# Rotary queries split in the projections and fetched into the operand's two tiles; five softmax buffers instead of six

## The chip, the cores and the metric

The kernel runs on one core of a Trainium2 chip. The metric is the device time of one execution in microseconds (us); lower is better. TensorE (PE) multiplies matrices, VectorE (DVE), ScalarE (ACT) and GpSimd (POOL) do the elementwise work, SyncE (SP) mostly issues transfers. Transfers can be issued from the queues of SP, ACT and POOL, and each engine works its own list of instructions in order; semaphores tie the lists together.

## The reference

One inference step of two decoder layers: the even layer mixes pooling and retention, the odd layer is multi-head latent attention, each is followed by a gated feed-forward network with a short convolution. There are 1024 prompt positions and 8 sample sequences of 4 new positions (1056 columns in all), model width 1024. The change concerns the attention layer: 8 heads, of which every query has a part of 128 without position and a rotary part of 64. The latent cache of a sample sequence holds 8192 old positions in 64 pages, and pages are found by a table. For the prompt, `q_pe` and `k_pe` are the rotary parts and `c_kv` the latent:

```
q_nope, q_pe, c_kv, k_pe = mla_project(...)      # rope on q_pe and k_pe
k_nope, v = c_kv @ w_uk, c_kv @ w_uv             # per head
s = (q_nope . k_nope + q_pe . k_pe) * MLA_SCALE   # causal
out = softmax(s) @ v, then w_o
```

For the samples the same sum runs over the cached pages, with `w_uk` folded into the query: scores against the 256 latent and 64 rotary columns of every cached row, softmax, and the latent rows weighted by it.

## The kernel before

The program is written by a planner in Python. Each piece of work is a generator (`heads`, `scores`, `outs`, `prepare`, `keys`, `values` and so on) that issues instructions and yields what it needs next: an event (`ev`), a buffer out of a stock (`res`), data that is ready (`rd`). `Pipe.run` (L470 on) keeps a clock model and always lets the task run that has the best priority among those that could start. So the instruction lists of all engines follow from the plan, and an edit that changes a stock, an event or a modelled cost moves other instructions too. A tile framework then adds the semaphores; transfers from SP and ACT share eight completion semaphores, taken in turn, and a transfer waits until the earlier one on its semaphore has landed.

Numbers of 32 bits are multiplied in two parts: `split` writes a rounded (high) part by a ScalarE cast and the rest (low) by a VectorE subtraction; a product then takes high x high, high x low and low x high. For the rotary queries the two parts are stacked: the operand `q2` of 128 rows holds the high part in rows 0 to 63 and the low part in rows 64 to 127.

*Projections* (`mla_proj`, about 1340 to 1410 us). `rotary(g)` makes the rotary queries of heads 4g to 4g+3: for three chunks of 352 columns it multiplies with the up-projection, rotates on VectorE and POOL and leaves the two halves of the rotary dimension in two tiles of `z`. Then, per head and half, the ACT queue stores 32 rows of 1056 columns into a DRAM tile `qpd` of 64 x 8 x 1056 (8 stores for each g, 16 in all, 132 KB each), because the rows of a head have to come to other partitions. `plain` makes the parts without position.

*Attention* (`attention`, about 1410 to 1990 us) runs two streams together. The samples: 352 page loads on SP and 160 gathers on POOL bring keys (`kt`), 128 gathers bring values (`vt`); products with them carry L632. The prompt, head by head: `heads` makes the keys of head h from `w_ukv` (loaded for every two heads, ACT queue), `scores` makes the scores of a block of queries, takes the maximum, the exponential (`p<-sc,amx` on ACT) and the scale (`p<-p,asm` on DVE); `outs` transposes p (L638), copies the transposed pieces to `th` and multiplies with `vv`. All 128 x 1024 buffers of this stream (p, raw weights, raw queries) come out of one ring of NP = 6 tiles, tag "p".

The rotary queries of head h come in `heads`: once head h-1 has been scored, a buffer of the ring is taken, two ACT-queue loads bring `qpd[:, h]` twice (rows 0 to 63 and again 64 to 127), the task waits until they are there, ACT casts all 128 rows into `q2`, and DVE overwrites rows 64 to 127 with the difference. At the start `load_queries` fetches those of head 0 (`qpe0`) and the last 32 columns of all heads (`qraw`) from SP's queue; DVE copies the latter into `qpS`, the rotary queries of the samples. L405 is the line of a helper that records every operation other than products, L616 that of the wide product.

Of the kernel before, what the change touches and what calls it, by code (L numbers as in the profile page):

```python
# [7 lines left out]
F32 = mybir.dt.float32  # L8
F32R = mybir.dt.float32r
# [8 lines left out]
SEQ = 1024  # L18
# [35 lines left out]
NP = 6  # L54
LAG = 1000.0
PL = 2
# [505 lines left out]
class Kernel:  # L562
# [727 lines left out]
    def mla_proj(self, src):  # L1290
# [130 lines left out]
        def rotary(g):  # L1421
# [4 lines left out]
            for c in range(3):  # L1426
# [15 lines left out]
                nc.gpsimd.tensor_tensor(o2[:, t0:t0 + n], o2[:, t0:t0 + n], ta, ALU.add)  # L1442
            self.done(("uqp", g))
            for hh in range(4):
                for half, o in ((0, o1), (1, o2)):
                    nc.scalar.dma_start(self.qpd[half * 32:half * 32 + 32, g * 4 + hh], o[hh * 32:hh * 32 + 32])
# [22 lines left out]
    def attention(self):  # L1469
# [9 lines left out]
        for shape, dtype, tag, bufs in (  # L1479
# [3 lines left out]
                ([128, 4, RW], F32, "mx", None), ([128, SEQ], F32R, "q2", 1),  # L1483
# [16 lines left out]
        ukv0, qpe0 = ptile(), ptile()  # L1500
        nc.sync.dma_start(ukv0, io["w_ukv"][0])
        nc.gpsimd.memset(qpS, 0.0)
        qraw = ptile()[:, :MH * NS].rearrange("p (h t) -> p h t", h=MH)

        def load_queries():

            for e in range(2):
                nc.sync.dma_start(qraw[64 * e:64 * e + 64], self.qpd[:, :, SEQ:])
            for e in range(2):
                nc.sync.dma_start(qpe0[64 * e:64 * e + 64], self.qpd[:, 0, :SEQ])  # L1510
            for e in range(2):
                s = slice(64 * e, 64 * e + 64)
                nc.vector.tensor_copy(qpS[s, :, e].rearrange("p b h i -> p h b i"), qraw[s].rearrange("p h (b i) -> p h b i", b=NB))
# [209 lines left out]
        pipe.stock("p", NP - 5)  # L1723
        hs = {}

        def heads():

            for h in range(MH):
                if h % 2 == 0:
                    if h:  # L1730
                        yield ("res", "p", 1)
                        raw = ptile()
                        nc.scalar.dma_start(raw, io["w_ukv"][h // 2])
                    else:
                        raw = ukv0
                    yield ("rd", raw)
# [25 lines left out]
                if h:  # L1762
                    yield ("res", "p", 1)
                    raw = ptile()
                    for e in range(2):
                        nc.scalar.dma_start(raw[64 * e:64 * e + 64], self.qpd[:, h, :SEQ])
                    yield ("rd", raw)
                else:
                    raw = qpe0
                q2 = ap.tile([128, SEQ], F32R, tag="q2", name="q2", bufs=1)  # L1770
                nc.scalar.copy(q2, raw)
                nc.vector.tensor_tensor(q2[64:128], raw[64:128], q2[64:128].bitcast(F32), ALU.subtract)
                pipe.give("p")
# [241 lines left out]
```

## Time and profile before

| | us |
|---|---|
| median of 3 runs | 2918.33 |
| lowest, highest | 2912.61, 2920.26 |
| profiled execution | 2925.62 |
| its span | 2923.8 |
| TensorE busy in the span | 2762.6 |
| attention, about 1410 to 1990 | 580 |

The span lies 1.8 us below its execution's time, and that execution is 7.3 us above the median. The mean granted TensorE clock of the span is 0.968 of full speed. In the rows, a start in us stands first, then a length, and in brackets the idle time of that engine just before, with what ended it.

### The profile page before, as it was taken

To read this page: it belongs to the slowest core of one execution; us is meant where nothing else is said; L and a number is where in the kernel's file an instruction comes from. 1 tells how busy PE (TensorE), PEld (TensorE's weight loads), DVE (VectorE), ACT (ScalarE), POOL (GpSimd) and SP (SyncE) were. 2 spreads that over 40 slices of the span, in tenths; PEclk is the share of its full clock that TensorE was granted. 3 is DMA by queue.
4 is the path that set the end of the run, shared out by engine and by line. 5 is a ranking of instruction groups with operands and counts; after the bars stand their busy time and mean duration, and the time that the engine had idled before them with its cause. 6 is when DMAs were issued, how large, how long until landed. Compare 5 with 4: busy or idle time off the path is not lost.

```text
span 2923.8 us, 44128 instructions
## 1 busy us (share of the span) xinstructions
PE 2762.6 (94%) x16897; PEld 2469.5 (84%) x16897; DVE 1421.2 (49%) x2720; ACT 868.1 (30%) x1833; POOL 755.0 (26%) x787
## 2 busy tenths in 40 slices
PE   8999998999999999899898988899889999999997
PEld 6777997999999999889654544478889999999996
DVE  4444547544444444764352534444674444444446
ACT  3322435211211222343332323243442211211224
POOL 1222334010111011323455665413420110111102
PEclk9999999999999999999998999889999999999997
DMA  3111421110211111122789999724211111111101
GB/s 135 60 59 46 117 82 34 55 47 30 66 44 44 44 51 46 44 99 83 244 291 298 334 348 347 266 95 146 73 44 37 51 51 29 63 47 44 51 25 60
DMA packets 136275, 301.81 MB, mean 103 GB/s; under 512 B 20960, under 2 KB 84240, under 8 KB 135936
## 3 DMA queue, kind: packets, MB, share of 16 engines
q1 hardware_dynamic: 89472, 175.35, 18.5%
q0 software_dynamic: 27968, 98.00, 9.6%
q10 hardware_dynamic: 18624, 25.63, 2.9%
q8 instruction: 134, 2.20, 0.3%
q14 instruction: 77, 0.63, 0.1%
HBM read 283.71 MB, written 15.21 MB: 102 GB/s over the span
## 4 chain that ended last, share of the span: by engine, by line
PE 79%; DVE 6%; DMA 5%; issue 5%; ACT 2%; POOL 2%; SPq 1%; ACTq 0%; DVEq 0%; POOLq 0%
PE bank L616 71%; PE bank L632 4%; DMA kt<-in_kT 3%; PE sc L616 2%; PE bank L638 2%; DVE ln_v L405 1%; DVE x L405 1%; DVE z L405 1%; DMA kt<-in_kT,kix 1%; DMA p<-qpd 1%; SPq L405 1%; DMA vt<-in_vrow,vix 1%; SPq L1914 1%; POOL z L405 1%; DVE wl L405 1%
## 5 line engine op out<-in xcount | busy, mean ns | idle before, releaser
L616 PE MATMUL bank<-x,wh 128*128 128x352 f32 x5664 | 1380.0, 327 | 19.3 <-DVE x L405 18.1
L616 PEld LDWEIGHTS bank<-x,wh 128*128 128x128 f32 x5664 | 992.8, 190 | 33.9 <-DVE x L405 23.3
L616 PE MATMUL bank<-x,wl 128*128 128x352 f32 x2832 | 915.2, 323 | 7.1 <-DVE wl L405 7.1
L616 PEld LDWEIGHTS bank<-x,wl 128*128 128x128 f32 x2832 | 537.4, 190 | 8.6 <-DVE wl L405 8.2
L405 ACT CAST wh<-wr 128x1024 fp32r<-128x1024 f32 (+1 forms) x196 | 202.6, 1041 | 668.7 <-PE bank L616 638.5
L405 DVE SCALAR_TENSOR_TENSOR z<-z,bank 128x352 f32<-128x352 f32 (+3 forms) x440 | 219.7, 513 | 326.7 <-PE bank L616 313.9
L616 PE MATMUL bank<-ah,wh 128*128 128x352 f32 (+3 forms) x1088 | 353.0, 324 | 0.0
L616 PE MATMUL bank<-ah,wl 128*128 128x352 f32 (+3 forms) x1088 | 350.9, 323 | 0.0
L616 PE MATMUL bank<-al,wh 128*128 128x352 f32 (+3 forms) x1088 | 350.6, 322 | 0.0
L405 POOL TENSOR_TENSOR wl<-wr,wh 128x1024 fp32r<-128x1024 f32 (+1 forms) x61 | 147.8, 2430 | 636.8 <-PE bank L616 391.6
L405 DVE TENSOR_TENSOR wl<-wr,wh 128x1024 fp32r<-128x1024 f32 (+1 forms) x137 | 175.7, 1284 | 147.2 <-ACT wh L405 142.5
L616 PE MATMUL bank<-wh,x 128*128 128x512 f32 (+3 forms) x720 | 239.5, 394 | 8.2 <-ACT wh L405 8.2
L616 PEld LDWEIGHTS bank<-ah,wh 128*128 128x128 f32 x1088 | 207.9, 191 | 1.2
L616 PEld LDWEIGHTS bank<-al,wh 128*128 128x128 f32 x1088 | 207.7, 191 | 1.2
L616 PEld LDWEIGHTS bank<-ah,wl 128*128 128x128 f32 x1088 | 207.9, 191 | 0.6 <-DVE wl L405 0.6
L405 POOL DMA_INDIRECT kt<-in_kT,kix x160 | 158.8, 992 | 133.3 <-DMA kt<-in_kT 53.4
L405 POOL COPY co<-a 128x2 f32<-128x2 f32 x44 | 39.2, 891 | 553.5 <-ACT a L405 553.5
L405 DVE SCALAR_TENSOR_TENSOR y<-a,prm,y 128x352 f32<-128x352 f32 (+1 forms) x264 | 166.1, 629 | 9.8
L405 DVE TENSOR_TENSOR g<-y,bank 128x352 f32<-128x352 f32 (+2 forms) x176 | 71.6, 427 | 202.7 <-PE bank L616 201.6
L405 DVE TENSOR_SCALAR y<-a,prm 128x352 f32<-128x352 f32 x132 | 79.1, 599 | 183.1 <-ACT a L405 177.6
L616 PEld LDWEIGHTS bank<-wh,x 128*128 128x128 f32 (+1 forms) x720 | 127.9, 182 | 32.6 <-ACT wh L405 8.2
L405 POOL DMA_INDIRECT vt<-in_vrow,vix x128 | 124.1, 970 | 102.7 <-PE bank L632 60.5
(234 smaller groups left out, 3215.9 us busy)
## 6 DMA issues: line engine op xcount, KB each, us to landing
kt<-in_kT SPq DMA_DIRECT2D x352, 160.0 KB
wr<-in_w_up SPq DMA_DIRECT2D x88, 512.0 KB
wr<-in_w_dn SPq DMA_DIRECT2D x44, 512.0 KB
wr<-in_w_h SPq DMA_DIRECT2D x16, 512.0 KB
wr<-in_w_oe SPq DMA_DIRECT2D x16, 512.0 KB
wr<-in_w_om SPq DMA_DIRECT2D x16, 512.0 KB
z<-in_xT SPq DMA_DIRECT2D x12, 352.0 KB
z<-in_xT ACTq DMA_DIRECT2D x3, 1408.0 KB
```

The source lines that it names most:

```text
L405: r = f(*args, **kw)
L616: self.nc.tensor.matmul(out, lhsT, rhs, start=start, stop=stop)
L632: self.nc.tensor.matmul(out[32 * g:32 * g + m], lhsT, rhs, start=start, stop=stop, tile_position=(0, 32 * g))
L638: self.nc.tensor.transpose(out, in_, self.ident[:in_.shape[0], :in_.shape[0]])
L1914: reg = nc.sync.value_load(entry, min_val=0, max_val=last)
```

## The change

`rotary(g)` now splits each rotated chunk at once: ACT casts and DVE subtracts, two times per chunk, into two tiles each of `xh` and `xl` (tiles of the activations that stand free there, whose memory the pools of attention take over later). The stores go from these, high rows into `qpd` rows 0 to 63 and low rows into 64 to 127; `qpd` is 128 x 8 x 1056 and there are 16 stores for each g, 32 in all, of 132 KB each. In attention, `load_q2(h)` is one ACT-queue load of 128 x 1024 straight into the operand `q2`, which has two buffers. The load for head 0 is issued when the task starts, that of head h+1 when head h begins. The cast, the subtraction, the raw buffer and the planner's wait are gone. `qraw` takes high and low parts (four loads of 64x8x32 instead of two), and DVE adds them into `qpS` instead of copying. The ring has five tiles, one of which is free at the start as before, and the planner lets the cast of a later `w_ukv` start 6000 ns after the time at which its model has the load ready (UKV).

```diff
--- before.py
+++ after.py
@@ -51,8 +51,9 @@
 NEV = 3
 PAIRS = (0, 1, 2, 3)
 NTH = 2
-NP = 6
+NP = 5
 LAG = 1000.0
+UKV = 6000.0
 PL = 2
 LNX = -1000.0
 SX = 400.0
@@ -1440,10 +1441,15 @@
                 self.drop(2)
                 nc.gpsimd.tensor_tensor(o1[:, t0:t0 + n], o1[:, t0:t0 + n], tb, ALU.subtract)
                 nc.gpsimd.tensor_tensor(o2[:, t0:t0 + n], o2[:, t0:t0 + n], ta, ALU.add)
+                yield True
+                for half, o in ((0, o1), (1, o2)):
+                    self.split(self.xh[:, 4 + 2 * g + half, t0:t0 + n], self.xl[:, 4 + 2 * g + half, t0:t0 + n], o[:, t0:t0 + n])
             self.done(("uqp", g))
             for hh in range(4):
-                for half, o in ((0, o1), (1, o2)):
-                    nc.scalar.dma_start(self.qpd[half * 32:half * 32 + 32, g * 4 + hh], o[hh * 32:hh * 32 + 32])
+                for part, x in ((0, self.xh), (64, self.xl)):
+                    for half in range(2):
+                        r = part + half * 32
+                        nc.scalar.dma_start(self.qpd[r:r + 32, g * 4 + hh], x[hh * 32:hh * 32 + 32, 4 + 2 * g + half].bitcast(F32))
 
         def plain(hp):
             wh, wl = yield from self.unit(("uqn", hp))
@@ -1480,7 +1486,7 @@
                 ([128, 1024], F32, "p", NP), ([128, 128], F32R, "qh", None),
                 ([128, 128], F32R, "ql", None), ([128, 4, VW], F32, "vt", VRAW),
                 ([128, 512], F32, "sev", NEV), ([128, 4, 4, RW], F32, "sT", NST),
-                ([128, 4, RW], F32, "mx", None), ([128, SEQ], F32R, "q2", 1),
+                ([128, 4, RW], F32, "mx", None), ([128, SEQ], F32R, "q2", 2),
                 ([128, SEQ], F32R, "kph", 1), ([128, SEQ], F32R, "kpl", 1), ([128, 512], F32R, "uh", 1),
                 ([128, 512], F32R, "ul", 1), ([128, 8, 256], F32, "vv", 1), ([128, 512], F32, "th", NTH),
                 ([128, 2, MH, NB, NQ], F32, "olT", 1),
@@ -1497,20 +1503,26 @@
         ukT = [ptile(), ptile()]
         for i in range(2):
             nc.sync.dma_start(ukT[i], io["w_ukT"][:, i * 1024:(i + 1) * 1024])
-        ukv0, qpe0 = ptile(), ptile()
+        ukv0 = ptile()
         nc.sync.dma_start(ukv0, io["w_ukv"][0])
         nc.gpsimd.memset(qpS, 0.0)
-        qraw = ptile()[:, :MH * NS].rearrange("p (h t) -> p h t", h=MH)
+        qraw = ptile()[:, :2 * MH * NS].rearrange("p (a h t) -> p a h t", a=2, h=MH)
+        q2s = {}
+
+        def load_q2(h):
+
+            q2 = q2s[h] = ap.tile([128, SEQ], F32R, tag="q2", name="q2", bufs=2)
+            nc.scalar.dma_start(q2.bitcast(F32), self.qpd[:, h, :SEQ])
 
         def load_queries():
 
             for e in range(2):
-                nc.sync.dma_start(qraw[64 * e:64 * e + 64], self.qpd[:, :, SEQ:])
-            for e in range(2):
-                nc.sync.dma_start(qpe0[64 * e:64 * e + 64], self.qpd[:, 0, :SEQ])
+                for a in range(2):
+                    nc.sync.dma_start(qraw[64 * e:64 * e + 64, a], self.qpd[64 * a:64 * a + 64, :, SEQ:])
             for e in range(2):
                 s = slice(64 * e, 64 * e + 64)
-                nc.vector.tensor_copy(qpS[s, :, e].rearrange("p b h i -> p h b i"), qraw[s].rearrange("p h (b i) -> p h b i", b=NB))
+                q = qraw[s].rearrange("p a h (b i) -> p a h b i", b=NB)
+                nc.vector.tensor_tensor(qpS[s, :, e].rearrange("p b h i -> p h b i"), q[:, 0], q[:, 1], ALU.add)
             pipe.give("p")
             pipe.fire("qps")
         for name, n in (("kt", KRAW), ("vt", VRAW), ("st", NST), ("ev", NEV)):
@@ -1720,20 +1732,23 @@
         nc.vector.tensor_copy(cmask, self.C("causal"))
         idb = ap.tile([128, 128], F32R, tag="idb", name="idb", bufs=1)
         nc.vector.tensor_copy(idb, self.ident)
-        pipe.stock("p", NP - 5)
+        pipe.stock("p", NP - 4)
         hs = {}
 
         def heads():
 
+            load_q2(0)
             for h in range(MH):
                 if h % 2 == 0:
                     if h:
                         yield ("res", "p", 1)
                         raw = ptile()
                         nc.scalar.dma_start(raw, io["w_ukv"][h // 2])
+                        pipe.fire(("ukv", h), self.clocks.ready(raw) + UKV)
+                        yield ("ev", ("ukv", h))
                     else:
                         raw = ukv0
-                    yield ("rd", raw)
+                        yield ("rd", raw)
                     wk = [ap.tile([128, 512], F32R, tag=t, name=t, bufs=1) for t in ("uh", "ul")]
                     self.split(*wk, raw[:, :512])
                     if h:
@@ -1759,18 +1774,9 @@
                     pipe.give("p", at=pipe.now)
                 if h:
                     yield ("ev", ("scored", h - 1))
-                if h:
-                    yield ("res", "p", 1)
-                    raw = ptile()
-                    for e in range(2):
-                        nc.scalar.dma_start(raw[64 * e:64 * e + 64], self.qpd[:, h, :SEQ])
-                    yield ("rd", raw)
-                else:
-                    raw = qpe0
-                q2 = ap.tile([128, SEQ], F32R, tag="q2", name="q2", bufs=1)
-                nc.scalar.copy(q2, raw)
-                nc.vector.tensor_tensor(q2[64:128], raw[64:128], q2[64:128].bitcast(F32), ALU.subtract)
-                pipe.give("p")
+                if h + 1 < MH:
+                    load_q2(h + 1)
+                q2 = q2s.pop(h)
                 kh = ap.tile([128, SEQ], F32R, tag="kph", name="kph", bufs=1)
                 kl = ap.tile([128, SEQ], F32R, tag="kpl", name="kpl", bufs=1)
                 for e in range(2):
@@ -1921,7 +1927,7 @@
         self.setup()
         self.drp = self.tc.alloc_tile_pool(name="dr", bufs=1, space=DRAM)
         xsp = self.drp.tile([128, 8, T], F32, name="xsp")
-        self.qpd = self.drp.tile([64, MH, T], F32, name="qpd")
+        self.qpd = self.drp.tile([128, MH, T], F32, name="qpd")
         self.open_x(True)
         self.drive(xsp)
         self.close_x()
```

The new lines shift the numbers by one: the helper's L405 reads L406 in the changed kernel. The order of ACT where the projections end and attention begins (`z<-bank` copies are those of `plain`, `x_81` and `x_82` are `xh` and `xl`, `q_...` is the operand `q2`); before:

```order
L405 DMA tab<-in_qtab 128x2x352 x2
L405 COPY z<-bank 128x352 x4
L405 DMA qpd<-z 32x1056 x8
L405 COPY z<-bank 128x352 x8
L405 CAST qh<-z 128x128 x2
L405 CAST uh<-p 128x512
L405 CAST wv<-p 128x512
L405 CAST q_12193<-p 128x1024
```

and now:

```order
L406 COPY z<-bank 128x352 x6
L406 CAST x_81<-z 128x352
L406 COPY z<-bank 128x352
L406 CAST x_81<-z 128x352
L406 DMA qpd<-x_81 32x1056 x2
L406 DMA qpd<-x_82 32x1056 x2
...
L406 COPY z<-bank 128x352 x5
L406 DMA q_12233<-qpd 128x1024
L406 DMA q_12869<-qpd 128x1024
L406 CAST qh<-z 128x128 x2
L406 CAST uh<-p 128x512
```

The stores of the second group (eight rows like the two shown, 16 stores) stand after seven copies instead of four, and behind the last splits; the loads of the first two operands follow them. In the middle of attention, ACT at the change from one head to the next (`p,asm<-sc,amx` are exponentials, `th` the transposed pieces), before:

```order
L405 ACTIVATE p,asm<-sc,amx 128x512 x2
L405 COPY z<-bank 128x256
L405 DMA p<-qpd 64x1024 x2
L405 COPY th<-bank 128x512 x2
L405 DMA p<-in_w_ukv 128x1024
L405 COPY th<-bank 128x512
L405 CAST q_15995<-p 128x1024
```

and now:

```order
L406 CAST qh<-z 128x128
L406 DMA q_15994<-qpd 128x1024
L406 ACTIVATE p,asm<-sc,amx 128x512 x2
L406 COPY th<-bank 128x256
L406 COPY th<-bank 128x128
L406 DMA p<-in_w_ukv 128x1024
```

The load moved from behind a head's last exponentials to ahead of them, and no cast of `q` follows. POOL at the start of attention, with its waits (`DMAHW` semaphores count transfers of SP and ACT), before:

```order
L405 MEMSET qpS 128x512
L405 DMA kt<-in_kT,kix_10697 128x320
```

and now:

```order
L406 MEMSET qpS 128x512 [waits DMAHW4_49,DMAHW3_49,DMAHW5_49,DMAHW1_49,DMAHW7_49,DMAHW0_49,DVE_49]
L406 DMA kt<-in_kT,kix_10697 128x320
```

The MEMSET got a wait for transfers, and the gathers of keys and values stand behind it as before.

## The prediction

> **What bounds the kernel now.** I read the page first, for the place of the attention stage in the span.
>
> ```profile
> span 2923.8 us, 44128 instructions
> PE 2762.6 (94%) x16897; PEld 2469.5 (84%) x16897; DVE 1421.2 (49%) x2720; ACT 868.1 (30%) x1833; POOL 755.0 (26%) x787
> ...
> DMA  3111421110211111122789999724211111111101
> ```
>
> TensorE is busy for 94% of the span, so only a stage in which it idles can give time. Each of the 40 slices is 73.1 us long; the DMA engines are full in slices 20 to 25, which is attention, about 1410 to 1990 us. The table of busy time by stretch gives that stage and some of its pieces (columns: length, then busy us and count of PE, PEld, DVE, ACT, POOL, then granted clock, DMA share, GB/s).
>
> ```profile
> 1410.00:1990.00 580.00, 505.97 (x3397) 308.84 (x3397) 245.07 (x624) 201.69 (x534) 290.16 (x294) 0.91 0.82 276
> 1530.00:1860.00 330.00, 286.95 (x1999) 164.64 (x1995) 132.25 (x334) 110.84 (x289) 187.92 (x191) 0.94 0.96 328
> ...
> 1530.00:1560.00 30.00, 23.44 (x138) 15.95 (x135) 8.25 (x17) 9.79 (x24) 16.15 (x15) 0.77 0.98 326
> 1680.00:1710.00 30.00, 22.32 (x156) 13.94 (x155) 7.45 (x15) 8.86 (x18) 13.69 (x15) 0.89 0.93 305
> 1740.00:1770.00 30.00, 28.94 (x196) 17.88 (x196) 16.01 (x50) 12.96 (x38) 20.94 (x22) 1.00 1.04 383
> 1770.00:1800.00 30.00, 24.68 (x186) 12.91 (x185) 10.71 (x22) 8.82 (x22) 16.12 (x16) 1.00 1.02 346
> 1830.00:1860.00 30.00, 25.22 (x178) 14.16 (x176) 12.59 (x31) 10.57 (x26) 9.20 (x10) 0.94 0.85 292
> 1855.00:1860.00 5.00, 2.79 (x10) 2.12 (x10) 2.54 (x5) 0.59 (x1) 0.00 (x0) 0.64 0.17 68
> ```
>
> TensorE idles for 580 - 506 = 74 us of the stage and runs below full clock at 0.91, while from 1530 to 1860 the DMA share is 0.96: two limits that change places. The waits of that stage (us in total, times, longest) tell what the rotary queries have to do with it.
>
> ```profile
> DVE q L405 <- ACT q L405: 59.1, 7, 15.5
> ACT q L405 <- DMA p<-qpd: 24.2, 6, 7.5
> PE bank L616 <- ACT th L405: 18.0, 8, 5.7
> ACT th L405 <- DMA kt<-in_kT: 11.2, 2, 7.4
> ACT z L405 <- DMA kt<-in_kT: 11.0, 2, 6.4
> ACT sT L405 <- DMA kt<-in_kT: 3.6, 1, 3.6
> PE bank L632 <- ACT pn L405: 3.6, 2, 3.3
> ACT p L405 <- DVE amx L405: 27.8, 24, 2.2
> ```
>
> Two kinds of wait stand here. ScalarE takes the rounded part (the cast `q<-p`) in its own order and stood 24.2 us for the load of a head's rotary queries. And three rows show it standing for a *cached-key* load, 25.8 us in five waits: in ScalarE's timeline each of these ends at the issue of an ACT-queue load (`p<-qpd`, `p<-in_w_ukv`), which shares its completion semaphore with a key load that has not landed. What TensorE felt of both is in its timeline (the bracket is its idle time before the row):
>
> ```profile
> 1540.58 2.07 PE L616 MATMUL bank<-th,vv 128*128 128x256 f32 x4 [4.29 <-ACT th L405]
> 1553.09 1.65 PE L616 MATMUL bank<-th,vv 128*128 128x256 f32 x4 [2.27 <-ACT th L405]
> ...
> 1683.00 1.13 PE L616 MATMUL bank<-th,vv 128*128 128x256 f32 x4 [1.93 <-ACT th L405]
> 1693.15 2.93 PE L616 MATMUL bank<-th,vv 128*128 128x256 f32 x6 [5.74 <-ACT th L405]
> ...
> 1782.22 1.13 PE L616 MATMUL bank<-th,vv 128*128 128x256 f32 x4 [0.83 <-ACT th L405]
> 1786.72 1.78 PE L616 MATMUL bank<-th,vv 128*128 128x256 f32 x8 [1.74 <-ACT th L405]
> ...
> 1857.21 0.37 PE L638 MATMUL bank<-ident,mxa 128*32 128x128 f32 x1 [4.78 <-DVE mxa L405]
> ```
>
> These seven are 21.6 us. The last is the low part's: VectorE's subtraction waited for the cast, and `mxa` stood behind it.
>
> **The change part by part.**
>
> *Attention body.* Per head it removes a cast, a subtraction and the wait for the load:
>
> ```profile
> L405 ACT CAST q<-p x8: 1028/1044/1048, 1413.0 to 1948.4; 128x1024 fp32r<-128x1024 f32 x8
> L405 DVE TENSOR_TENSOR q<-p,q x8: 1222/1222/1223, 1417.7 to 1949.5; 64x1024 fp32r<-64x1024 f32 x8
> ```
>
> That is 8 x 1.04 = 8.4 us of ScalarE and 8 x 1.22 = 9.8 us of VectorE, engines busy 202 and 245 of 580 us, so only the waits count. Removable on TensorE: 21.6, and 3.3 behind `pn` (the `w_ukv` load), together 24.9 us. Behind the stalls the clock falls: (1 - 0.77) x 23.4 + (1 - 0.89) x 22.3 + (1 - 0.94) x 25.2 = 5.4 + 2.5 + 1.5 = 9.4 us in the three windows that hold them. Gross 34.3.
>
> Not all of it is time. The bytes stay (a head was two loads of 64x1024, now one of 128x1024, 512 KB either way), and where the DMA is full a faster TensorE only waits for keys. I count in full what fell where the DMA was idle or had room: the stall at 1857 with its clock (4.78 + 1.5; the share there was 0.17) and the 3.3, together 9.6. The other six stalls, 16.8 us with 7.9 of clock, lie in the windows 1530, 1680 and 1770 with shares 0.98, 0.93 and 1.02, mean 0.977; the fullest window reached 1.04, so they leave 0.063 x 90 = 5.7 us. Body: 9.6 + 5.7 = 15.3. Against it: ACT-queue loads do not vanish. There were 14 + 3 of them after the start, now there are 6 + 3, and the new ones stand ahead of the last two exponentials of a head, so whoever waits on a shared semaphore holds up the probabilities, then the transposes, then `th`. Before, 17 loads cost TensorE 4.29 + 1.93 + 0.83 + 3.3 = 10.4; 9/17 of it is 5.5, and at the same discount (15.3/34.3) 2.5. Bounds 0 and 10.4. Body: **-13** (bounds 0 and -26.7, the latter 24.9 - 5.5 + 7.3 of clock).
>
> The Trainium skill ("TensorE: Matmul & The Clock Gate", section "What's actually happening") says the clock halves after an idle window of about 3.4 us and returns after as long a busy one. By that rule, the estimate for three stalls above 3.4 us is 3 x 1.7 = 5 us instead of 9.4. The 0.77 of the window at 1530 agrees that stalls are followed by a low clock, and costs more than the rule.
>
> *The start of attention.* The splits themselves are 12 casts and 12 subtractions of 128x352, near the `z` copies of that shape (0.45 us, below); ScalarE idled 23.56 us there, so they hide. The stores do not:
>
> ```profile
> 1388.71 0.45 ACT L405 COPY z<-bank 128x352 f32<-128x352 f32 x1 [23.56 <-PE bank L616]
> 1394.44 4.15 ACTq L405 DMA_DIRECT2D qpd<-z  x8
> ...
> 1406.88 2.60 SPq L405 DMA_DIRECT2D p<-qpd  x4
> ...
> 1390.70 0.53 POOL L405 MEMSET qpS<- 128x512 f32 x1
> 1409.79 0.94 POOL L405 DMA_INDIRECT vt<-in_vrow,vix  x1 [10.52 <-PE bank L616]
> 1416.05 0.94 POOL L405 DMA_INDIRECT kt<-in_kT,kix  x1 [0.30 <-issue]
> ...
> 1421.92 1.92 PE L632 MATMUL bank<-kt,qlT 128*32 128x512 f32 x4 [4.96 <-DMA kt<-in_kT,kix]
> ```
>
> Eight stores took 4.15 us of the ACT queue, 0.52 each; SP saw the last land at 1406.88. Sixteen take 8.3, and in the new order they stand three copies and two splits later. With 1.9 us from copy to copy (1388.71 to 1394.44 are three) I put the first at 1400.7, the last issue at 1409 and the last landing at 1411 to 1414. Three queues are late with them. SP holds `w_ukT`, `w_ukv`, `p<-qpd`, `kix` and all page loads behind them. POOL's MEMSET of `qpS` now waits until the split tiles are stored, because their memory is reused, so three key and two value gathers that were issued between 1391 and 1399 go behind it. From MEMSET to the sixth key gather (the one that TensorE waited for) stand 3 + 5 + 2 gathers of 1.25 us apart and the MEMSET, 13.1 us: with the MEMSET at 1412 the gather comes at 1425 instead of 1416.05. **+10** for this and for the fuller queue (bounds +4, if the stores land within 1 us; +14, if the first keys also carry what the early gathers had moved). If that cover, the projections' matmuls to 1413, were gone, it would be all of the 13.
>
> The Trainium skill ("DMA: Bandwidth & Descriptors", section "Queues, rings and completion order") says that every DMA engine takes turns between queue rows packet by packet. By that, stores and `w_uk` loads halve each other and the landing is the late one, +14. The trace agrees in that eight stores issued by 1398.6 were seen only at 1406.88.
>
> `qpS` now comes from four loads and two additions (before, two copies of a quarter of a microsecond), behind the same load: nothing, or the fraction of a microsecond. The fifth softmax buffer: the exponentials waited for `amx`, never for a buffer, and one buffer fewer stands against one that no raw query takes: 0, bounds 0 and +5. The `w_ukv` cast placed 6 us after its load by the plan: 0.
>
> *The end.* The first output weights wait for the last value product now, not for VectorE's late `ql`, and come some 50 us earlier, so POOL's splits no longer fall beside the last softmax:
>
> ```profile
> 1977.49 2.73 DVE L405 TENSOR_SCALAR p<-p,asm 128x1024 f32<-128x1024 f32 x1
> ...
> 1980.28 1.54 PE L638 MATMUL bank<-ident,p 128*128 128x128 f32 x6 [2.76 <-DVE p L405]
> ```
>
> 2.76 us of TensorE and about 1.2 of clock behind it: **-4** (bounds 0 and -5).
>
> *Sum* against the profiled execution, 2925.6 (span 2923.8): -13 + 10 - 4 = -7, 2918.6. That execution lies 7.3 above the median 2918.3, so the median after is **2911**, 0.25% below. What a measurement can tell from no change is about 0.3%, 8.8 us: 2909.6 and 2927.1.
>
> **Rivals.** *A: all waits turn into time.* Body -26.7, start +4, tail -4: -27, **2891**. For it: at 1740 the DMA moved 383 GB/s against 328 on average, so there is room if buffers come free evenly. Against it: the shares near 1.0 in two of the three windows.
>
> *B: the keys take over.* The removed waits come back at `kt` and `vt`, body -3, +10, -4: **2921**. For it: 0.96 over 330 us. Against: the stall at 1857, with an idle DMA.
>
> *C: slower; the new load in front of the exponentials.* A load of the next head that waits for a key load now stops ScalarE in the middle of a softmax. It decides when at least three of the six loads catch a key load in flight: 3 x 25.8/5 = 15.5 us on TensorE, 3 of clock, start +14, no tail gain, less 15: +17.5, **2936**. For it: in the order, the key buffer whose load shares the semaphore was released only 17 to 126 TensorE instructions ahead, and the two longest waits before came at short leads. Against: most leads are longer than 70.
>
> *D: it does not do what it says* has little room: no `q<-p` cast remains in the order.
>
> **How the numbers follow.** Forecast 0.40 (own range 2903 to 2919), A 0.25, B and D 0.15, C 0.20. Below 2909.6: A and 0.17 of the forecast, 0.42. Above 2927.1: C and 0.04 of B, 0.24. Between: 0.34. Range 2887 to 2934, from A nearly to C's price, leaving about a tenth at each side.
>
> **What would show it.** After: no row `q<-p`; `PE bank L616 <- ACT th` from 18.0 to below 9; first `bank<-kt` later than 1428; SP's `p<-qpd` after 1411; no 2.7 us `p<-p,asm` at the end. A is right if the stage is shorter than 560 us from first keys; B if the waits `<- DMA kt` or `vt` of TensorE grow by 10 us; C if a row `ACT p <- DMA kt` appears with over 10 us. I am wrong if the stores land as before (start +0), or if the planner's shifted order loses more than these terms.

## The result and the profile after

The changed kernel takes 2901.22 us in the median of 7 runs (2896.43 to 2907.46), against 2919.43 for the kernel before, run beside it. The ratio is 0.9943 (95% interval 0.9929 to 0.9956): 16.6 us faster by the ratio, 18.2 between the medians. I had forecast 2911, a gain of 7.

The page of the changed kernel answers to the one shown before:

```profile
span 2903.2 us, 44119 instructions
PE 2750.1 (95%) x16897; PEld 2457.8 (85%) x16897; DVE 1420.9 (49%) x2724; ACT 865.4 (30%) x1837; POOL 754.7 (26%) x787
...
DMA  3111420211110211122779999953111110211101
```

The span is 20.6 us shorter. To see where, one has to find the seams of the stage. The rows of a tile give each group's first and last start. For the key products (`kt`) and the value products (`vt`) of the samples, before:

```profile
L632 PE MATMUL bank<-kt,qlT x512: 589/592/1062, 1421.9 to 1850.8; 128*32 128x512 f32 x171
L632 PE MATMUL bank<-vt,sT x1024: 380/380/637, 1478.0 to 1930.4; 128*32 128x257 f32 x171
```

and after:

```profile
L633 PE MATMUL bank<-kt,qlT x512: 589/592/1062, 1438.6 to 1866.2; 128*32 128x512 f32 x171
L633 PE MATMUL bank<-vt,sT x1024: 378/380/637, 1498.9 to 1929.5; 128*32 128x257 f32 x171
```

The stream of cached pages starts 16.7 us later and ends 0.9 us earlier. What is left of attention behind the last value product is prompt work, but for 38 products that end the samples, the same in both (`dr<-ol`, `olT,uvn`, `ol,cst`). The first product of the output projection ends it, at 1989.33 before and here after:

```profile
1970.83 1.05 PE L617 MATMUL bank<-x,wh 128*128 128x352 f32 x3 [1.21 <-ACT x L406]
```

So the leftover is 1989.3 - 1930.4 = 58.9 us before and 1970.8 - 1929.5 = 41.3 after. The table of busy time for exactly these two stretches, before:

```profile
1930.40:1989.30 58.90, 49.70 (x267) 41.97 (x260) 25.57 (x73) 26.21 (x73) 7.58 (x8) 0.88 0.14 45
```

and after:

```profile
1929.50:1970.80 41.30, 35.46 (x223) 30.59 (x215) 20.36 (x59) 19.43 (x57) 7.59 (x8) 1.00 0.11 40
```

TensorE has 223 products left instead of 267, and the granted clock is 1.00 instead of 0.88. The DMA share is 0.14 and 0.11, so the stream of pages is over there, and the 17.6 us of difference are time. The account of the span is then:

- Ahead of attention: 4.9 us later. The projections end at 1409.5 before and 1414.4 after, and 4.7 of it stand already at one stall (`[1.03 <-DVE wl]`, at 1337.51 and 1342.25) in code that is not changed.
- Start of attention: 11.8 us longer. From the end of the projections to the first key product it is 12.4 and 24.2.
- Stream, from first key to last value product: 508.5 and 490.9, 17.6 us shorter.
- Leftover: 17.6 us shorter.
- Everything behind: 934.5 and 932.4, 2.1 us shorter.

The sum is 4.9 + 11.8 - 17.6 - 17.6 - 2.1 = -20.6. Stream and leftover together, before and then after:

```profile
1421.92:1989.33 567.41, 498.93 (x3361) 304.33 (x3361) 238.55 (x610) 198.38 (x526) 280.98 (x285) 0.92 0.82 275
```

```profile
1438.60:1970.83 532.23, 482.90 (x3360) 291.89 (x3361) 231.19 (x603) 191.50 (x519) 278.04 (x285) 0.96 0.85 292
```

Of the 35.2 us, 16.0 are busy time of TensorE (the same products at a granted clock of 0.96 instead of 0.92), and 19.2 are idle time of TensorE (68.5 and 49.3).

TensorE's waits for keys and values in this stage before (us, times, longest):

```profile
PE bank L632 <- DMA vt<-in_vrow,vix: 12.1, 11, 1.9
PE bank L632 <- DMA kt<-in_kT,kix: 10.5, 2, 5.5
PE bank L632 <- DMA kt<-in_kT: 7.8, 5, 3.7
```

The waits of the stage after, TensorE's first:

```profile
PE bank L633 <- DMA kt<-in_kT,kix: 16.0, 3, 9.2
PE bank L633 <- DMA kt<-in_kT: 14.8, 4, 5.6
PE bank L617 <- ACT th L406: 12.1, 7, 3.5
...
PE bank L633 <- DMA vt<-in_vrow,vix: 2.5, 5, 1.0
...
PE bank L639 <- DVE mxa L406: 0.4, 1, 0.4
...
ACT p L406 <- DMA kt<-in_kT: 16.3, 4, 5.3
ACT sev L406 <- DMA kt<-in_kT: 8.8, 1, 8.8
ACT uh L406 <- DMA p<-in_w_ukv: 6.6, 1, 6.6
```

ScalarE no longer waits for rotary queries. Its waits for key loads that share a semaphore are 25.1 us, as many as before (25.8), with nine issues instead of seventeen. TensorE's wait for `th` fell by 5.9 us, that for `mxa` by 6.2 (from 6.6) and that for `pn` by all of its 3.6: 15.7 us together, against the 24.9 that I had meant to remove and the 35.2 by which the stage is shorter. Whether they went because of the removed work and the early fetch is what the experiments ask.

### The profile page after: what moved, and what is told of

Its sections match the earlier page's. It is cut to its first block, busy times and chain, and to the rows that moved or that the text cites. A ratio compares the mean times of both kernels' runs of the same rounds, so it can differ in the third digit from the quotient of the medians.

```text
span 2903.2 us, 44119 instructions
## 1 busy us (share of the span) xinstructions
PE 2750.1 (95%) x16897; PEld 2457.8 (85%) x16897; DVE 1420.9 (49%) x2724; ACT 865.4 (30%) x1837; POOL 754.7 (26%) x787
## 4 chain that ended last, share of the span: by engine, by line
PE 79%; DVE 6%; issue 5%; DMA 4%; POOL 2%; ACT 2%; SPq 2%; ACTq 0%; DVEq 0%; POOLq 0%
PE bank L617 71%; PE bank L633 4%; PE sc L617 2%; DMA kt<-in_kT 2%; PE bank L639 2%; DVE x L406 1%; DVE ln_v L406 1%; DVE z L406 1%; SPq L406 1%; POOL z L406 1%; DMA vt<-in_vrow,vix 1%; SPq L1920 1%; DMA kt<-in_kT,kix 1%; DVE wl L406 1%; DVE ln_r L406 0%
## 5 line engine op out<-in xcount | busy, mean ns | idle before, releaser
L406 ACT CAST wh<-wr 128x1024 fp32r<-128x1024 f32 (+1 forms) x196 | 202.6, 1041 | 669.8 <-PE bank L617 637.9
L406 DVE SCALAR_TENSOR_TENSOR z<-z,bank 128x352 f32<-128x352 f32 (+3 forms) x440 | 219.7, 512 | 320.7 <-PE bank L617 310.9
L406 POOL TENSOR_TENSOR wl<-wr,wh 128x1024 fp32r<-128x1024 f32 (+1 forms) x61 | 147.9, 2433 | 662.1 <-PE bank L617 391.6
L406 DVE TENSOR_TENSOR wl<-wr,wh 128x1024 fp32r<-128x1024 f32 (+1 forms) x137 | 175.7, 1284 | 147.6 <-ACT wh L406 142.9
L406 POOL DMA_INDIRECT kt<-in_kT,kix x160 | 156.2, 976 | 133.7 <-PE bank L633 50.4
L406 POOL COPY co<-a 128x2 f32<-128x2 f32 x44 | 39.3, 892 | 553.7 <-ACT a L406 553.7
L406 DVE SCALAR_TENSOR_TENSOR y<-a,prm,y 128x352 f32<-128x352 f32 (+1 forms) x264 | 166.2, 629 | 9.8
L406 DVE TENSOR_TENSOR g<-y,bank 128x352 f32<-128x352 f32 (+2 forms) x176 | 71.6, 428 | 199.5 <-PE bank L617 198.4
L406 DVE TENSOR_SCALAR y<-a,prm 128x352 f32<-128x352 f32 x132 | 77.9, 590 | 184.1 <-ACT a L406 178.6
L406 POOL DMA_INDIRECT vt<-in_vrow,vix x128 | 124.2, 971 | 85.6 <-PE bank L633 52.4
```

The source lines that it names most:

```text
L406: r = f(*args, **kw)
```

## The experiments

Twelve runs, on four chips; the chip of the two kernels' first runs is not on record. The kernel before takes 2998 and 2989 us on chips 15 and 6, and 2917 and 2915 us on chips 3 and 8, near the 2919 of the result. So times are compared by the ratio to the kernel before on the same chip. The fourth column counts the rows of TensorE's order that are not the changed kernel's; the last two come from the traces as above.

One limit of the traces matters below. On chips 15 and 6, 65 to 107 us of ScalarE's idle time in the stage have no named cause (rows `<- remote` and `<- issue`); on the others it is 1.4 us at most. A wait by name from chips 15 and 6 is therefore a lower bound.

| run | chip | ratio, interval | rows of TensorE's order that differ | last value product | leftover, us |
|---|---|---|---|---|---|
| kernel before | - | 1 | 510 | 1930.4 | 58.9 |
| changed kernel | - | 0.9943, 0.9929 to 0.9956 | 0 | 1929.5 | 41.3 |
| e14_onebuf | 3 | 0.9939, 0.9917 to 0.9961 | 4 | 1920.1 | 45.7 |
| e16_late_work | 8 | 0.9944, 0.9922 to 0.9966 | 14 | 1928.7 | 41.4 |
| e12_pool2 | 3 | 0.9954, 0.9938 to 0.9971 | 0 | 1924.9 | 43.0 |
| e17_big_same | 8 | 1.0086, 1.0061 to 1.0111 | 0 | 1967.5 | 41.4 |
| before_again | 6 | 1.0013, 0.9996 to 1.0030 | 510 | 1993.2 | 55.6 |
| after_again | 6 | 0.9936, 0.9910 to 0.9963 | 0 | 1990.0 | 42.7 |
| e1_work | 15 | 0.9932, 0.9908 to 0.9956 | 28 | 1994.8 | 45.7 |
| e5_ukv | 6 | 0.9931, 0.9904 to 0.9957 | 35 | 1982.9 | 41.4 |
| e8_q2pool | 15 | 0.9938, 0.9917 to 0.9959 | 25 | 2001.0 | 43.1 |
| e9_bigpool2 | 6 | 0.9959, 0.9944 to 0.9975 | 508 | 2004.2 | 32.1 |
| e2_late | 15 | 0.9995, 0.9976 to 1.0015 | 563 | 1997.0 | 63.3 |
| e3_big | 15 | 1.0001, 0.9981 to 1.0021 | 508 | 2026.3 | 30.7 |

### Is it the removed work, or the early fetch?

The first pair takes back one half of the change each. *e1_work* keeps the early fetch and puts a cast and a vector operation of the old sizes back:

```diff
                 q2 = q2s.pop(h)
+                yield ("rd", q2)
+                nc.scalar.copy(q2, q2.bitcast(F32))
+                nc.vector.tensor_tensor(q2[64:128], q2[64:128].bitcast(F32), q2[64:128].bitcast(F32), ALU.max)
```

> The changed kernel with the work per head put back, the fetch left early: when a head begins, ScalarE casts the operand of 128x1024 in place (1.04 us) and VectorE takes the maximum of its lower 64 rows with themselves (1.22 us), both the identity, 8 times each, and the plan waits for the load as before the change. Theory (the early fetch gives the gain): the cast finds its data there, so the time stays within 4 us of the changed kernel, 2901 to 2905, and no row of ScalarE waits for a load of the rotary queries. Rival (the removed cast and subtraction give it): half or more of the 18 us comes back, 2910 or more.

Measured 0.9932 (0.9908 to 0.9956); the changed kernel's own ratio is 0.9936 on chip 6 and 0.9943 in the result. The work costs nothing that these runs can show. One part of the expectation failed: ScalarE did wait for the fetches,

```profile
ACT q L406 <- DMA q<-qpd: 15.5, 5, 6.4
```

15.5 us in five waits, half of it (7.8) at the first two heads, and the time did not care.

*e2_late* issues the fetch of head h where head h begins and lets the plan wait for it:

```diff
-                if h + 1 < MH:
-                    load_q2(h + 1)
+                if h:
+                    load_q2(h)
                 q2 = q2s.pop(h)
+                yield ("rd", q2)
```

> The changed kernel with the fetch made late again: the load of head h is issued only when head h-1 is scored and the plan waits for it, as before the change; no cast, no subtraction, one load instead of two. Theory (early fetch): TensorE's products of a head then wait for the load and its neighbours, and half or more of the gain is lost, 2910 to 2917. Rival (removed work): 2901 to 2905. A third possibility: without a cast in ScalarE's list nothing but the scores themselves needs the operand, and making the head's keys (about 15 us) covers the load, so that late costs nothing either: then neither early fetch nor work alone is needed, only that no cast stands in the list behind the load.

Measured 0.9995 (0.9976 to 1.0015): the whole gain is gone. I first took this as proof of the early fetch. The trace says otherwise. ScalarE's issues of the first two fetches after the start, in this run:

```profile
1517.92 0.33 ACTq L406 DMA_DIRECT2D q<-qpd  x1
...
1593.14 0.33 ACTq L406 DMA_DIRECT2D q<-qpd  x1
```

and in the changed kernel on chip 6:

```profile
1523.97 0.33 ACTq L406 DMA_DIRECT2D q<-qpd  x1
...
1592.89 0.35 ACTq L406 DMA_DIRECT2D q<-qpd  x1
```

They are the fetches of heads 2 and 3 in both, and they are no later. Measured from issue to the first product that uses the operand, the seven fetches behind the first lead by 87 to 140 us in e2_late and by 90 to 138 in after_again (before: 14 to 62). In e2_late each of the last six was issued within 6 us behind the last product that reads its buffer, two heads ahead, and not where the program text has it. So the edit did not make the fetch late. What did change is TensorE's order, in 563 rows, because the plan waited. The leftover, next to that of e1_work on the same chip:

```profile
1997.00:2060.30 63.30, 54.66 (x301) 46.19 (x293) 28.37 (x83) 27.77 (x81) 7.58 (x8) 0.92 0.07 28
```

```profile
1994.80:2040.50 45.70, 40.14 (x224) 34.68 (x216) 20.48 (x59) 19.63 (x57) 7.57 (x8) 0.89 0.11 37
```

The stream is equally long in the two (560.9 and 560.4 us). The 17.6 us of leftover are nearly all of the 20.1 us between their medians (2997.2 and 2977.0).

### The same order with the old waits

*e14_onebuf* makes the fetch late in the data, by one operand buffer instead of two, and keeps the plan as it was (the helper reckons with two buffers, and a second tile is reserved unused):

```diff
-                ([128, 4, RW], F32, "mx", None), ([128, SEQ], F32R, "q2", 2),
+                ([128, 4, RW], F32, "mx", None), ([128, SEQ], F32R, "q2", 1), ([128, SEQ], F32R, "q2pad", 1),
...
-            q2 = q2s[h] = ap.tile([128, SEQ], F32R, tag="q2", name="q2", bufs=2)
...
+                q2 = ap._real.tile([128, SEQ], F32R, tag="q2", name="q2", bufs=1)
...
```

> The changed kernel with one buffer for the operand instead of two, the plan told nothing of it (a second tile of that size is reserved and unused): TensorE's order and the other engines' are the changed kernel's row for row, but ScalarE's list has each fetch one head later, where the last scores of the head before free the buffer. In the variant with the fetch placed late by the program, the list had been put in order again by what the data allow, so that its fetches were no later than the changed kernel's, while its TensorE order differed in some 770 rows; its loss of the whole gain may thus be the order's. Theory A (early fetch gives the gain): TensorE waits at the first scores of each head, more than 25 us over seven heads, ratio to before 0.998 to 1.003. Theory B (the order that the plan wrote without the wait gives it): 0.992 to 0.996, as the changed kernel.

0.9939 (0.9917 to 0.9961): theory A, mine until then, is out. The fetches are late indeed: they lead by 14 to 47 us, as in the kernel before (14 to 62), where the changed kernel has 88 to 124. TensorE's waits for `th` are 11.9 us, and none of its larger waits names a fetch. (The "some 770 rows" of the expectation are 563, see the table.)

*e16_late_work* has both halves of the old scheme, the late fetch (by the edit just shown) and work of the old sizes behind it in the lists of ScalarE and VectorE, with the plan told of neither (the two operations are issued past the plan's clock model):

```diff
+                nc.scalar._real.copy(q2, q2.bitcast(F32))
+                nc.vector._real.tensor_tensor(q2[64:128], q2[64:128].bitcast(F32), q2[64:128].bitcast(F32), ALU.max)
```

> The changed kernel with both halves of the old scheme back and the plan told of neither: one operand buffer, so that each fetch is late (as in the run with one buffer), and the cast of 128x1024 in place and the maximum of 64 rows behind it (as in the run with the work put back), in the lists of ScalarE and VectorE where the old cast and subtraction stood. TensorE's order differs from the changed kernel's in some 14 rows. Each half alone kept the gain (0.9939 and 0.9932). Theory B (the order that the plan wrote gives the gain): the ratio stays at 0.992 to 0.996, although ScalarE waits more than 15 us for fetches. Theory C (the old cast loses only because its fetch is late, so that either half mends it): 0.998 to 1.002.

0.9944 (0.9922 to 0.9966). This is the run that decides, and three groups of its rows show it: the waits, the value products, and the leftover.

```profile
ACT q L1788 <- DMA q<-qpd: 29.4, 8, 7.4
...
PE bank L617 <- ACT th L406: 11.4, 8, 2.7
```

```profile
L633 PE MATMUL bank<-vt,sT x1024: 378/380/637, 1497.4 to 1928.7; 128*32 128x257 f32 x171
```

```profile
1928.70:1970.10 41.40, 35.55 (x224) 30.62 (x216) 20.84 (x60) 19.53 (x57) 7.54 (x8) 1.00 0.14 43
```

ScalarE waits 29.4 us for fetches (22.0 behind the first head; before, 24.2 and 22.8), and yet stream (1437.2 to 1928.7, 491.5 us) and leftover (41.4) are the changed kernel's. The late fetch, the cast and the subtraction did not cost the 18 us by themselves: with the fetch late and operations of these sizes behind it, TensorE's stalls behind `th` did not return (11.4 against 18.0). The order that the plan wrote around them did. The other half of this is e2_late: there the fetch is early, the work is gone and the buffers and stores are the new ones, and with another order the gain is gone.

Two limits belong to it. ScalarE's waits for all these transfers (fetches, keys, `w_ukv`) are 50.0 us before, 31.7 in the changed kernel and 36.9 in e16, because its waits for key loads fell to 1.7 when the fetch waits came back; so e16 does not show that 50 us of them would be free. And the order of e2_late is not the kernel before's (463 rows differ); a run with exactly the old order and the new transfers was not made. What e16 does not put back is the raw buffer and the ring of six, the second load and the old stores. From the code I take it that the line `yield ("rd", raw)` and the modelled load and cast made the difference, since they keep the planner from starting a head's keys until its model has the load in. Two runs narrow this down: e1_work has the line and the modelled cast with an early load, and 28 rows of the order change; e2_late has the line with a load that the plan issues late, and 563 change. So in e2_late it is the plan's waiting for a late load. That it is the same in the kernel before is inferred; the raw buffer and the ring of six, which the plan knows too, were not tried alone. Shown is what came of it: at the end of the stream 223 or 224 products are left under this order, 267 under the old one and 301 in e2_late. The place of the last head says the same. Its first product with the operand `q2` starts 6.5 us behind the last value product in the changed kernel and in every run whose order differs from it by at most 35 rows, whatever the chip; it starts 25.0 and 26.4 us behind in the two traces of the kernel before, and 28.6 in e2_late. How the order also shortens the stream by 17.6 us, no run shows.

### The plan's other edit

*e5_ukv* takes the 6000 ns back (`yield ("rd", raw)` in place of the timed event).

> The changed kernel, with the later w_ukv casts placed when the plan's model has the load ready (as before the change) instead of 6000 ns after. If the 6000 ns carry part of the gain, ScalarE waits longer than 6.6 us for w_ukv and the time is 3 us or more above the changed kernel's; by my prediction (0) it is within 2 us of it.

0.9931 (0.9904 to 0.9957), not to be told from after_again's 0.9936. The edit is worth nothing that these runs can show, as I had put it. The ScalarE wait for `w_ukv` is 7.6 us there and 9.7 in after_again (lower bounds both).

For that comparison, and for the traces of both kernels on a slower chip, they were run as they are:

> The changed kernel itself beside the next three, so that what follows is compared on one chip; the chip of the four runs before this one moved the keys more slowly (258 GB/s in the stage against 292). If the gain is of the mechanism and not of one chip, the ratio to the kernel before is 0.992 to 0.996 here too. From the early-fetch theory, the variant with the work put back (0.9932) was then equal to it.

> The kernel before itself, for its trace on this chip: the ratio is 1. Where the chip moves keys more slowly, TensorE's waits for keys are longer than the 18.3 us of the first trace, and the waits for transposed pieces (18.0 us) and ScalarE's for the rotary queries (24.2 us) are about as they were.

(The "one chip" of the first text is chip 6; the four runs before it were on chip 15.) Both ratios came out as expected. The picture of the waits did not: TensorE of the kernel before waited 6.6 us for SP's key loads there (7.8 in the first trace) and 25.3 for `th`. With 27.4 us of TensorE's idle time unnamed in that trace, it cannot say where the slower stream shows.

### Shared semaphores, and the start

*e8_q2pool* issues the fetches from POOL (`nc.gpsimd.dma_start` in `load_q2`).

> The changed kernel with the eight fetches of the rotary queries issued from POOL's queue instead of ScalarE's, so that they share no completion semaphore with the key loads of SP. Theory (shared semaphores still cost): ScalarE's 25 us of waits for key loads fall to those at the weight loads (below 10), TensorE's waits for the transposed pieces fall below 12.1, time 2892 to 2898. Rival (the keys limit the stage): the waits for key loads on TensorE rise by as much, 2899 to 2904. Against both: a gather queue that stands behind a fetch whose buffer is not free, slower than 2905.

0.9938 (0.9917 to 0.9959): no gain over the changed kernel, as the rival had it. The rival's mechanism is not shown. ScalarE's list has no wait for a key load any more, and TensorE's waits for key loads are 24.0 us where e1_work on the same chip has 13.8; but 106.9 us of ScalarE's idle time and 29.5 of TensorE's have no name in this trace.

*e3_big* stores 128 x 1056 at once, from a DRAM tile ordered by part, half, head and row:

```diff
-            for hh in range(4):
-                for part, x in ((0, self.xh), (64, self.xl)):
-                    for half in range(2):
-                        r = part + half * 32
-                        nc.scalar.dma_start(self.qpd[r:r + 32, g * 4 + hh], x[hh * 32:hh * 32 + 32, 4 + 2 * g + half].bitcast(F32))
+            for part, x in ((0, self.xh), (2, self.xl)):
+                for half in range(2):
+                    nc.scalar.dma_start(self.qpd[part + half, g * 4:g * 4 + 4].rearrange("h i t -> (h i) t"), x[:, 4 + 2 * g + half].bitcast(F32))
...
```

> The changed kernel with 8 stores of 128x1056 instead of 32 of 32x1056 (same bytes; the DRAM tile is ordered by part, half, head, row, so a tile is stored as it lies; the fetch of a head is one load still, the last 32 columns of all heads come in eight small loads instead of four). Theory (the stores' issue and their turns on the shared semaphores hold up the start): ScalarE's wait of 9.4 us for a store goes, the stores land before 1408 and the first product with gathered keys comes 12 to 16 us after the last projection instead of 24.2, time 2889 to 2894. Rival (the start is bound by the bytes, or by the memory that stores and gathers share): within 3 us of the changed kernel, 2898 to 2904.

1.0001 (0.9981 to 1.0021): the whole gain is gone, which neither side had expected. The stores did land early, POOL's MEMSET ran at 1402.89. But SP stood over its eight small loads, and all page loads stand behind them. My reading was that two of them share semaphores with the first two fetches, which landed late:

```profile
1402.78 36.46 SPq L406 DMA_DIRECT2D p<-qpd  x8
1439.28 0.45 SPq L406 DMA_DIRECT2D kix<-in_ptb  x1
```

*e9_bigpool2* adds to e3_big the first two fetches on POOL's queue, with semaphores of their own:

```diff
-            nc.scalar.dma_start(q2.bitcast(F32), self.qpd[:, h, :, :SEQ])
+            (nc.gpsimd if h < 2 else nc.scalar).dma_start(q2.bitcast(F32), self.qpd[:, h, :, :SEQ])
```

> The variant with 8 stores of 128x1056, and the fetches for heads 0 and 1 issued from POOL's queue, so that no load of SP shares a completion semaphore with them. In the variant with 8 stores alone POOL began at 1402.9 instead of 1418.8, but SP stood 36 us over its eight small loads, two of which wait for those fetches. Theory (the semaphores shared with the first fetches cost that start): SP issues the eight loads within 6 us, the first key product comes below 16 us after the first product with w_uk (20.0 in the changed kernel), and the time is 6 to 10 us below that of the changed kernel. Rival (the bytes or gathers limit the start): no more than 2 us below.

```profile
1406.02 4.50 SPq L406 DMA_DIRECT2D p<-qpd  x8
1410.57 0.45 SPq L406 DMA_DIRECT2D kix<-in_ptb  x1
```

36.46 us became 4.50, and the first key product came 9.4 us after the first `w_uk` product instead of 22.6 in after_again: the start was held by the semaphores, as expected. But the ratio is 0.9959 (0.9944 to 0.9975), no better than the changed kernel's 0.9936 on that chip (the intervals overlap). An earlier start did not reach the end. The order of e9 and e3, with 508 rows changed, has the shortest leftovers (32.1 and 30.7 us), and in e9 a longer stream (582.1 us against 551.1 in after_again), so a short leftover alone is not a gain.

*e12_pool2* has the same two fetches on POOL in the changed kernel, with its 32 stores and its TensorE order.

> The changed kernel with the fetches for heads 0 and 1 issued from POOL's queue: TensorE's order is the same row for row, the 32 stores and the layout too. With 8 stores and these two fetches on POOL the first key product came 9.4 us after the first w_uk product instead of 22.6, and the stage still ended later: its first 330 us moved 243 GB/s instead of 257. If the DRAM layout or the stores were to blame, this one has the changed kernel's stage and gains a little at the start (kix no longer waits for a fetch): 2 to 5 us below it, ratio 0.992 to 0.993. If an earlier start as such gives nothing, the ratio stays at 0.9936 within its interval.

0.9954 (0.9938 to 0.9971): the first key product came 16.6 us after the first `w_uk` product (changed kernel 20.0), and nothing was gained (e14_onebuf has 0.9939 on the same chip). *e17_big_same* puts the 8 stores under the changed kernel's order, by telling the plan's model of the old transfers:

> The changed kernel with 8 stores of 128x1056 and the first two fetches on POOL's queue (the variant whose stage began 13 us earlier but took 20 us longer), now with the plan told of the 32 stores and the old loads, so that TensorE's and VectorE's orders are the changed kernel's row for row; in the earlier variant 510 rows of TensorE's order differed. Theory B (the order decides how long the stage takes): the early start is kept, first key product 9 to 12 us after the first w_uk product, the stage from there as long as in the changed kernel, time 6 to 11 us below it, ratio 0.990 to 0.992. Rival (the DRAM layout or an early start makes the stage longer): as the earlier variant or the changed kernel, 0.994 to 0.996.

1.0086 (1.0061 to 1.0111), slower than the kernel before. Theory B was wrong here in its second half: the order is not all. The start is early, but TensorE's second group of keys waited:

```profile
1420.48 1.92 PE L633 MATMUL bank<-kt,qlT 128*32 128x512 f32 x4 [1.92 <-DMA kt<-in_kT]
1441.06 3.41 PE L633 MATMUL bank<-kt,qlT 128*32 128x512 f32 x12 [16.24 <-DMA kt<-in_kT,kix]
```

So the second group comes at 1441.06, about when the changed kernel has its first (1438.60). And the stream ends late although the leftover is as short as the order makes it (41.4). The first 330 us of this stream and of that of e16_late_work on the same chip:

```profile
1420.48:1750.48 330.00, 268.67 (x1705) 152.97 (x1706) 115.89 (x301) 100.96 (x268) 155.66 (x162) 0.90 0.87 267
```

```profile
1437.20:1767.20 330.00, 299.13 (x1989) 172.20 (x1990) 142.00 (x359) 119.32 (x313) 181.62 (x185) 0.94 0.91 306
```

267 GB/s at a share of 0.87 against 306 at 0.91. SP stood 17.9 us for fetches in this run. I have not shown whether the layout of the DRAM tile makes the fetches slow, or what else lowers the rate; that stays open, and with it whether the changed kernel's 11.8 us at the start can be won. No run beat the changed kernel by more than the intervals allow.

## Why the prediction was right and where not

The sign and the range held, the reason did not.

*Attention body, -13.* The step that failed is "Removable on TensorE: 21.6, and 3.3". I read seven idle times of TensorE that ended at ScalarE or VectorE, put them down to the late fetch, the cast and the subtraction, and took them as time that comes back when these go. e16_late_work has the late fetch and work of the same sizes back, and the stalls stay away (`th` 11.4 us against 18.0, `mxa` 3.3 against 6.6) and the gain stays. The stalls were real, but they came with the order that the plan had written, and so did the leftover.

The second wrong step is the discount. I called the DMA full at a share of 0.96 and allowed 5.7 of 24.7 us. From 1530 to 1860 us the changed kernel moved 338 GB/s at a share of 0.97 where the kernel before moved 328 at 0.96, and the whole stream became 17.6 us shorter with the same pages. So the share was no ceiling. Before the discount I had 34.3 us for the body and 4 for the end, near the 35.2 that were measured. That is luck, since the waits that I named were not the cause, and the clock's part was 16.0 and not 9.4.

Third, of the two 17.6 us one lies behind the stream, where I had looked only at the last softmax. The rows for it were in the trace of before: the DMA share of 0.14 over 58.9 us says that prompt work was left over.

*Start, +10.* The mechanism was right. MEMSET came at 1418.83 and not 1412, most of it because all of the start lay 4.9 us later: the first of the second group's 16 stores went at 1404.97 and not at 1400.7, and the 16 took 9.3 us and not 8.3. The first key product came 11.8 us later behind the projections, in the bounds. Whether these 11.8 us are lost at the end is doubtful after e9, e12 and e17.

*End, -4.* Right in what it named: the longest `p<-p,asm` fell from 2727 to 874 ns.

```profile
L406 DVE TENSOR_SCALAR p<-p,asm x64: 278/534/874, 1475.2 to 1963.3; 128x128 f32<-128x128 f32 x8, 128x256 f32<-128x256 f32 x8, 128x384 f32<-128x384 f32 x8, 128x512 f32<-128x512 f32 x8
```

It is a part of the 17.6 us of the leftover. Its clock term is not shown: the clock of the leftover rose from 0.88 to 1.00, but e14_onebuf has 0.89 there (1920.1 to 1965.8) and no `p<-p,asm` above 866 ns.

*Nothing for UKV.* Shown by e5_ukv. *Nothing for the fifth buffer* was not tried alone.

*Rivals.* A's sign came (532.2 us from first keys, below 560), but not by its mechanism. C's sign came as well, `ACT p <- DMA kt` with 16.3 us, but its price of 15.5 us on TensorE did not: the waits for `th` fell to 12.1. B's sign did not come: TensorE's waits for `kt` behind the first keys went from 13.3 us (10.5 + 7.8 less 5.0 at the first) to 21.6 (16.0 + 14.8 less 9.2), and those for `vt` from 12.1 to 2.5. "The planner's shifted order loses more than these terms" stood in the last sentence of the prediction as a way to be wrong. The order was in fact what carried the gain, so with the other sign, and it had no price at all.

## What to carry to other kernels

Where a planner writes the order, price an edit first by what it does to the plan: find the point where the long transfer stream ends, and count the products that each order has left behind it (267 before, 223 after, 301 in e2_late). Read the length of the stream beside it: e9_bigpool2 left 32.1 us and gained nothing by it, and e17_big_same has the changed kernel's order and was slower than the kernel before. A stall with a named releaser need not belong to that releaser; hold the order fixed and put the wait back to find out. And an experiment that edits a planned program has to be compared row for row in its order before its time is read as the effect of the edit.

## What was not expected of the hardware

The same program took 2968 us on chip 6 and 2901 us in the result's runs. The stretch from the output projection to the end is the same (933.5 and 932.4 us), and that from the first key product to the output projection is 593.8 against 532.2, with 261 against 292 GB/s:

```profile
1438.90:2032.67 593.77, 506.15 (x3361) 303.46 (x3361) 229.40 (x603) 190.32 (x519) 275.34 (x284) 0.93 0.79 261
```

```profile
1438.60:1970.83 532.23, 482.90 (x3360) 291.89 (x3361) 231.19 (x603) 191.50 (x519) 278.04 (x285) 0.96 0.85 292
```

The effect of the change is the same on both (0.9936 and 0.9943). Why the chips differ, no run shows. And in e3_big SP stood 36.46 us over eight small loads, against 4.50 in e9_bigpool2, where two fetches of other data no longer shared its semaphores: which transfers share a semaphore is a resource of its own.
